# Five buffers in place of three for the raw halves of w_in's weights

## The chip, the core and the metric

The kernel runs on one core of a Trainium2 chip. The core has a matrix engine (PE, TensorE), a vector engine (DVE), a scalar engine (ACT), GpSimd (POOL) and a sync engine (SP), which here only issues transfers. Each takes its instructions in the order in which they stand in its own queue. A transfer is issued by SP's or ACT's queue and then carried out by 16 DMA engines that all queues share. The fast memory on the chip, SBUF, has 128 partitions; a buffer of it is given by its bytes per partition. The metric is the time of one execution in microseconds (us), as the median of several runs.

## The reference

One layer of a decoder for a prompt of 1024 rows and 64 sample rows (eight sequences of eight), with 1024 channels. It normalizes x and conditions it, projects it once, sends the parts of the projection through a pooling branch and a state-space (SSD) branch, and merges the two:

```python
shift, scale, gate = split(silu(c) @ w_ada + b_ada, 3)
h = rmsnorm(x, norm_g) * (1 + scale) + shift
u_pool, z_pool, z_ssm, xbc, dt_raw, g_raw = split(h @ w_in)     # one projection
p = (pool_mix(u_pool) * silu(z_pool)) @ w_pool_out
xs, B, C = split(silu(causal_conv(xbc)))
y = ssd(xs, softplus(dt_raw + dt_bias), -exp(a_log), B, C, state) + d_skip * xs
s = rmsnorm(y * silu(z_ssm), ssm_norm_g) @ w_ssm_out
m = sigmoid(g_pool) * p + sigmoid(g_ssm) * s
out = rmsnorm(x + gate * (m @ w_o), final_g)
```

All inputs and outputs are float32. The new states of pooling, convolution and SSD are outputs as well.

## The kernel before

**The projection.** h @ w_in is computed with h transposed: 1088 columns (1024 prompt rows and 64 sample rows), in halves of 544 and quarters of 272. The output channels of w_in go in pairs of 128 columns. Each pair is a two-by-two block product, carried out in the manner of Strassen with seven block products in place of eight (`strassen`). The blocks of the weight, b11, b12, b21 and b22, are the two halves of the 1024 input channels by the two column blocks of the pair.

**The loads in question.** For a pair, `pair_w` loads two raw tiles with the tag "rawA", one for each half of the input channels: 128 partitions by 4 KB. If the two column blocks are neighbours, a tile is one transfer of 512 KB (line 541); if not, two of 256 KB (line 544). They are issued by SP's queue. From the blocks, DVE and POOL make sums and differences (line 555; two more tiles with the tag "raw", called t3 and t2, and some in place in rawA). Each of the seven operands is then split into two parts of lower width that the matmul takes: ACT copies the high half (`whi`, line 166) and POOL, in the opening DVE, subtracts for the low half (`wlo`, line 169). `product` multiplies high by high, high by low and low by high, 128x272 each (lines 609 to 611), into PSUM, and DVE adds the results up (lines 620 and 625; tiles s1, u2, u3 and c2).

**Slots.** Tiles with one tag and in one pool take turns in a fixed number of buffers. The load of tile n waits until every reader of tile n-3 has finished; which is POOL's last wlo of it, as a rule. A load that waits on SP's queue holds up what stands behind it there: the stores of presplit weights (below), loads of convolution state (stc), of initial states, of the weights for the gate.

**The stages.** `first` makes the opening, up to about 107 us in the profile: x is loaded, its squares are summed (`x_square`, which uses a rawA tile as scratch), silu(c) @ w_ada gives the conditioning (`ada_out` uses a rawA tile too), h is made, and the first pair of the projection runs inside it. Its order is written out by hand. Then come the other pairs, to about 828 us, woven with their followers: convolution units (line 1057 on DVE), pooling units, outputs to DRAM through ACT (lines 721 and 723: activation and store). Beside them, a function `prep` splits the weights w_pool_out and w_ssm_out ahead of time: ACT's queue loads a block (pw, line 427, two buffers), ACT scales it (line 435) and makes the high half (ph, line 436), POOL the low half in place (line 438), and SP stores that (line 442, ws<-pw or wp<-pw). The last ten pairs run beside the SSD of the samples. The chunk stage, about 828 to 1178 us, works on the prompt's SSD in chunks of 128 rows. The tail applies w_o.

**What sets the order.** Outside the opening, a scheduler places each engine's instructions by priorities and by simulated times, in which the number of buffers counts. The order that results is fixed in the program.

**The pool.** rawA lies in the pool `pa`, with raw, s1, u2, u3, c2 and others, at the left end of SBUF; each tag follows the last one used before it. When the pairs are done, `pa` is closed and the pools of the chunk stage, `cl` and `ck`, are opened on the space. A tile of a new pool that lies on a tile of the old one waits for the last use of it: the framework adds the waits that are needed, one by one. In the chunk stage `ck` holds, among others, bt and btl (high and low half of B transposed, lines 1417 and 1444), xd and xw, xwl (x times dt; x times a decay in high and low half, lines 1426, 1429 and 1445), two of each.

Of the kernel before, what the change touches and what calls it, by code (L numbers as in the profile page):

```python
# [8 lines left out]
F32 = mybir.dt.float32  # L9
# [11 lines left out]
P = 128  # L21
D = 1024
# [24 lines left out]
def tile_pool_ssd_step(  # L47
# [9 lines left out]
    def nm(s):  # L57
        uid[0] += 1
        return f"{s}_{uid[0]}"
# [9 lines left out]
    def open_(name, bufs, side="left"):  # L69
        cm = tc.tile_pool(name=name, bufs=bufs, side=side, reuse_waits="tile")  # L70
        kept.append(cm)
        return cm.__enter__()
# [10 lines left out]
    pa = open_("pa", 1)  # L83
# [6 lines left out]
    def R(shape=(P, T), dt=F32):  # L90
        return hs.tile(list(shape), dt, tag="R", name=nm("R"), bufs=3)
# [71 lines left out]
    def split(raw, kept=None, ncols=P, eng=None):  # L163
        hi = wp.tile([P, 4, P], F32R, tag="whi", name=nm("whi"), bufs=4)
        lo = wp.tile([P, 4, P], F32R, tag="wlo", name=nm("wlo"), bufs=4)
        ins = act(hi[:, :, :ncols], raw[:, :, :ncols], AF.Copy)  # L166
        if kept is not None:
            kept.append(ins.ins)
        (eng or nc.gpsimd).tensor_tensor(lo[:, :, :ncols], raw[:, :, :ncols], hi[:, :, :ncols].bitcast(F32), ALU.subtract)  # L169
        return hi, lo  # L170

    def raw_(shape=(P, 4, P)):
        return pa.tile(list(shape), F32, tag="raw", name=nm("raw"), bufs=RAW)
# [28 lines left out]

    def x_square(i, eng):
        xt, n = xr[i]
        sqj = pa.tile([P, D], F32, tag="rawA", name=nm("sqj"), bufs=3)
        if eng is V:
            V.scalar_tensor_tensor(sqj[:n], xt[:n], 1.0, xt[:n], ALU.mult, ALU.mult, accum_out=ss[:n, i:i + 1])
        else:
            act(sqj[:n], xt[:n], AF.Square, accum_out=ss[:n, i:i + 1])
# [70 lines left out]
    def ada_out(part):  # L280
        a, b = PARTS[part]
        n = (b - a) * P // 2
        mr = pa.tile([P, 256], F32, tag="rawA", name=nm("mr"), bufs=3)
        act(mr[:, :n], pm[part][:, :n], AF.Copy)
        return mr

# [246 lines left out]
    def pair_w(c0, c1, pri, early):  # L533
        def run():
            with tc.high_priority(pri):
                raws = []
                for j in range(2):
                    r = pa.tile([P, 4, 2, P], F32, tag="rawA", name=nm("rawA"), bufs=3)
                    rows_ = w_in[0, j * 512:(j + 1) * 512]
                    if c1 == c0 + P:  # L540
                        load(r, rows_[:, c0:c0 + 2 * P].rearrange("(k p) (t c) -> p k t c", p=P, c=P))
                    else:
                        for t, c in enumerate((c0, c1)):
                            load(r[:, :, t], rows_[:, c:c + P].rearrange("(k p) c -> p k c", p=P))
                    raws.append(r)
            b11, b12, b21, b22 = raws[0][:, :, 0], raws[0][:, :, 1], raws[1][:, :, 0], raws[1][:, :, 1]
            w = []

            def add(x):
                with tc.high_priority(pri):  # L550
                    w.append(split(x, highs, eng=V if early else None))

            def diff(dst, x, y, op=ALU.subtract, eng=V):
                with tc.high_priority(pri):
                    eng.tensor_tensor(dst, x, y, op)  # L555

            def first_steps():
                t3, t2 = raw_(), raw_()
                diff(t3, b22, b12)
                diff(t2, t3, b11, ALU.add)  # L560
                yield
                add(b11)
                add(b21)
                diff(b21, t2, b21)
                yield
                add(b21)
                add(t2)
                yield
                add(t3)
                yield  # L570
                diff(b12, b12, b11)
                add(b12)
                yield
                add(b22)
                yield

            def steps():
                t3, t2 = raw_(), raw_()
                diff(t3, b22, b12)
                yield  # L580
                diff(t2, t3, b11, ALU.add)
                add(t2)
                add(t3)
                yield
                diff(b12, b12, b11)
                add(b12)
                add(b21)
                diff(t2, t2, b21, eng=nc.gpsimd)
                add(t2)
                add(b22)  # L590
                yield
            if early:
                return w, first_steps()
            add(b11)
            prep_q.append(steps())
            return w, prep_q[-1]
        return run
# [262 lines left out]
    def first():  # L860
# [51 lines left out]
        late = late_loads()  # L912

        x_square(0, V)
        x_square(1, V)
        c_turn()
        x_root(0, 2)
        x_unit(0, 2)
        x_square(2, None)
        x_square(3, V)  # L920
        x_turns(0, range(2))
# [21 lines left out]
        ada_mm(0, 6)  # L943
        ada_mm(0, 7)
        mr = ada_out(0)
        x_turns(2, range(5, 6))
        ada_end(0, mr)
# [15 lines left out]
        for k in range(4, 8):  # L963
            ada_load(2, k)
        next(late)
        mr = ada_out(1)
        products(2, range(1))
        ada_end(1, mr)
# [11 lines left out]
        for k in range(4, KT):  # L980
            ada_mm(2, k)
        mr = ada_out(2)
        products(2, range(3, 4))
        dtw = dt_w()
# [998 lines left out]
    for i in range(8):  # L1983
# [4 lines left out]
        r = R((P, D))  # L1988
# [65 lines left out]
```

## Time and profile before

| | |
|---|---|
| runs | 1292.78, 1290.96, 1286.81 us; median 1290.96 |
| profiled execution | 1292.2 us, its span 1290.4 us |
| mean granted clock of PE | 0.995 |
| 0 to 107 us (opening) | PE 95.26 of 107.00 us busy |
| 107 to 400 us (pairs) | PE 288.87 of 293.00 |
| 400 to 828 us (pairs, samples) | PE 420.67 of 428.00 |
| 828 to 1178 us (chunks) | PE 344.45 of 350.00 |
| 1178 to 1290 us (tail) | PE 105.83 of 112.00 |

The runs spread over 6 us. In the table the last five rows are from the windows of the trace. In rows of the timeline the columns are the start in us, the duration, the engine (with a q: its queue, for a transfer that it issues), the line, the operation, output<-inputs and, in square brackets, the idle time before it on its engine with what ended that. In rows of waits they are the waiting engine and line, what it waited for, and the total in us, the number of waits and the longest, or, for PE, the mean. A row of windows has the stretch, its length, busy us of PE, PE's weight loads, DVE, ACT and POOL with the number of instructions, the granted clock of PE, the share of the DMA engines and GB/s.

### The profile page before, as it was taken

How to read it: one execution, taken by the hardware profiler on the slowest of the kernel's cores; microseconds unless marked ns; L12 is line 12 of the kernel's file. 1: busy time of each engine (PE TensorE's matmuls, PEld its weight loads, DVE VectorE, ACT ScalarE, POOL GpSimd, SP SyncE). 2: the span in 40 equal slices, each digit the busy share in tenths (PEclk: the TensorE clock that was granted, in tenths of full speed). 3: DMA queues.
4: the chain of work that ended last, by engine and by line, in shares of the span. 5: the costliest groups of instructions: out<-in, count | busy, mean ns of one | idle time of the engine just before them, and what ended most of it. 6: DMA issues, size and time to landing. Idle time of an engine off the chain costs nothing. (4 is left out here: it accounts for less than half of the span.)

```text
span 1290.4 us, 26363 instructions
## 1 busy us (share of the span) xinstructions
PE 1255.1 (97%) x9771; PEld 1176.8 (91%) x9771; DVE 911.8 (71%) x1584; ACT 718.4 (56%) x1685; POOL 675.5 (52%) x555
## 2 busy tenths in 40 slices
PE   7999999999999999999999999999999999999997
PEld 6779999989999999999889999989999999989786
DVE  4686778865979588776667665488667879767533
ACT  4665356465556655554554564686887768522211
POOL 1007658678869777564344443446465656636000
PEclk9999999999999999999999999999999999999999
DMA  9736354465456453444546555889666666575431
GB/s 329 243 116 220 117 164 160 143 198 178 142 164 219 144 184 126 152 154 121 160 134 202 168 155 157 288 289 317 221 197 184 185 215 207 161 270 181 158 105 50
DMA packets 225730, 234.90 MB, mean 182 GB/s; under 512 B 30370, under 2 KB 177010, under 8 KB 225595
## 3 DMA queue, kind: packets, MB, share of 16 engines
q1 hardware_dynamic: 155808, 159.01, 39.6%
q10 hardware_dynamic: 69794, 74.22, 16.8%
q8 instruction: 77, 1.26, 0.4%
q14 instruction: 51, 0.41, 0.1%
HBM read 158.67 MB, written 74.62 MB: 181 GB/s over the span
## 5 line engine op out<-in xcount | busy, mean ns | idle before, releaser
L169 POOL TENSOR_TENSOR wlo<-rawA,whi 128x512 fp32r<-128x512 f32 x120 | 186.8, 1561 | 186.6 <-ACT whi L166 102.0
L169 POOL TENSOR_TENSOR wlo<-raw,whi 128x512 fp32r<-128x512 f32 x92 | 149.4, 1631 | 125.1 <-ACT whi L166 120.7
L360 PE MATMUL mm<-Y,whi 128*128 128x352 f32 (+1 forms) x480 | 160.0, 333 | 2.7 <-DVE G L1890 2.5
L361 PE MATMUL mm<-Y,whi 128*128 128x352 f32 (+1 forms) x480 | 157.8, 329 | 0.4 <-DVE Y L1516 0.4
L362 PE MATMUL mm<-Y,wlo 128*128 128x352 f32 (+1 forms) x480 | 157.3, 328 | 0.0
L611 PE MATMUL mm<-Y,wlo 128*128 128x272 f32 x496 | 143.7, 290 | 4.1 <-POOL wlo L169 3.6
L609 PE MATMUL mm<-Y,whi 128*128 128x272 f32 x496 | 146.4, 295 | 0.3 <-ACT whi L166 0.2
L609 PE MATMUL ps<-Y,whi 128*128 128x272 f32 x496 | 144.4, 291 | 2.2 <-ACT o L809 1.6
L610 PE MATMUL ps<-Y,whi 128*128 128x272 f32 x496 | 143.1, 289 | 0.0
L610 PE MATMUL mm<-Y,whi 128*128 128x272 f32 x496 | 142.8, 288 | 0.0
L611 PE MATMUL ps<-Y,wlo 128*128 128x272 f32 x496 | 142.6, 288 | 0.0
L166 ACT ACTIVATE whi<-rawA 128x512 fp32r<-128x512 f32 x125 | 78.0, 626 | 97.9 <-PE ps L610 43.2
L1057 DVE SCALAR_TENSOR_TENSOR GA<-GA,cvT,GA 128x1112 f32<-128x1112 f32 x72 | 126.4, 1758 | 0.3
L166 ACT ACTIVATE whi<-raw 128x512 fp32r<-128x512 f32 x96 | 58.8, 626 | 90.7 <-DVE raw L555 39.3
L611 PEld LDWEIGHTS mm<-Y,wlo 128*128 128x128 f32 x496 | 93.4, 188 | 6.0 <-POOL wlo L169 4.9
L609 PEld LDWEIGHTS ps<-Y,whi 128*128 128x128 f32 x496 | 93.3, 188 | 3.7 <-ACT o L809 1.8
L360 PEld LDWEIGHTS mm<-Y,whi 128*128 128x128 f32 x480 | 90.6, 189 | 5.5 <-DVE G L1890 3.5
L609 PEld LDWEIGHTS mm<-Y,whi 128*128 128x128 f32 x496 | 93.3, 188 | 2.4 <-ACT whi L166 0.9
L610 PEld LDWEIGHTS mm<-Y,whi 128*128 128x128 f32 x496 | 93.4, 188 | 0.7 <-issue 0.6
L610 PEld LDWEIGHTS ps<-Y,whi 128*128 128x128 f32 x496 | 93.3, 188 | 0.3 <-issue 0.2
L611 PEld LDWEIGHTS ps<-Y,wlo 128*128 128x128 f32 x496 | 93.5, 188 | 0.2 <-issue 0.2
L361 PEld LDWEIGHTS mm<-Y,whi 128*128 128x128 f32 x480 | 90.5, 189 | 2.6 <-DVE Y L1516 0.9
(459 smaller groups left out, 3842.8 us busy)
## 6 DMA issues: line engine op xcount, KB each, us to landing
rawA<-in_w_in SPq DMA_DIRECT2D x46, 512.0 KB
dec<-acs_d SPq DMA_DIRECT2D x32, 512.0 KB
xbc<-GA ACTq DMA_DIRECT2D x24, 512.0 KB
xb<-xbc SPq DMA_DIRECT2D x32, 384.0 KB
rawA<-in_w_in SPq DMA_DIRECT2D x32, 256.0 KB
pw<-in_w_ssm_out ACTq DMA_DIRECT2D x32, 256.0 KB
ws<-ph ACTq DMA_DIRECT2D x32, 256.0 KB
ws<-pw SPq DMA_DIRECT2D x32, 256.0 KB
```

The costliest lines, as they stand in the source:

```text
L166: ins = act(hi[:, :, :ncols], raw[:, :, :ncols], AF.Copy)
L169: (eng or nc.gpsimd).tensor_tensor(lo[:, :, :ncols], raw[:, :, :ncols], hi[:, :, :ncols].bitcast(F32), ALU.subtract)
L360: mm(ps[:, :n], a, rh[k][:, o:o + n], start=(k == 0), stop=False)
L361: mm(ps[:, :n], a, rl[k][:, o:o + n], start=False, stop=False)
L362: mm(ps[:, :n], b, rh[k][:, o:o + n], start=False, stop=(k == nk - 1))
L609: mm(p, hi, ah, start=(k == 0), stop=False)
L610: mm(p, hi, al, start=False, stop=False)
L611: mm(p, lo, ah, start=False, stop=(k == 3))
L1057: V.scalar_tensor_tensor(d[:, :n], rp[:, k:k + n], cvT[:, 24 * k + mc:24 * k + mc + 1], d[:, :n], ALU.mult, ALU.add)
```

## The change: five buffers for the tag rawA

The number of buffers of the tag "rawA" goes from 3 to 5, in the three places that name it. The same transfers, copies and products are made of the same sizes.

```diff
@@ x_square
-        sqj = pa.tile([P, D], F32, tag="rawA", name=nm("sqj"), bufs=3)
+        sqj = pa.tile([P, D], F32, tag="rawA", name=nm("sqj"), bufs=5)
@@ ada_out
-        mr = pa.tile([P, 256], F32, tag="rawA", name=nm("mr"), bufs=3)
+        mr = pa.tile([P, 256], F32, tag="rawA", name=nm("mr"), bufs=5)
@@ pair_w
-                    r = pa.tile([P, 4, 2, P], F32, tag="rawA", name=nm("rawA"), bufs=3)
+                    r = pa.tile([P, 4, 2, P], F32, tag="rawA", name=nm("rawA"), bufs=5)
```

Load n now waits for the readers of tile n-5. The pool `pa` grows by 8 KB per partition; the pools that are open beside it keep their places. What the scheduler makes of it is seen in the order of the queues. The number at a tile's name tells its instances apart.

On SP's queue, where the loads of the second and third pair stand in the opening (L839 are the gate's weights; rawA_1301 and rawA_1303 are the second pair's halves, rawA_1309 and rawA_1312 the third's):

```order
 L839 DMA gk_730<-in_w_ada 128x1024
 L541 DMA rawA_1301<-in_w_in 128x4x256
+L541 DMA rawA_1303<-in_w_in 128x4x256
+L544 DMA rawA_1309<-in_w_in 128x4x128 x2
 L839 DMA R_823<-in_w_ada 128x1024
 L839 DMA R_829<-in_w_ada 128x1024
```

Before, these two stood nine rows later, behind the gate's weights and other loads. Further on, too, each rawA load stands about two loads earlier; around 495 to 543 us of the profile, on SP's queue (ws<-pw are the stores of presplit weights):

```order
 L541 DMA rawA_6878<-in_w_in 128x4x256
 L442 DMA ws_213<-pw_6727 128x512
+L541 DMA rawA_7471<-in_w_in 128x4x256
 L442 DMA ws_214<-pw_6864 128x512
-L541 DMA rawA_7471<-in_w_in 128x4x256
+L541 DMA rawA_7473<-in_w_in 128x4x256
 L442 DMA ws_215<-pw_7039 128x512
+L541 DMA rawA_7479<-in_w_in 128x4x256
 L442 DMA ws_216<-pw_7176 128x512
-L541 DMA rawA_7473<-in_w_in 128x4x256
-L541 DMA rawA_7479<-in_w_in 128x4x256
```

The loads moved ahead of the stores ws_214, ws_215 and ws_216, by one store or two. On DVE, in the opening, the three differences of the second pair (raw_1323 is its t3, raw_1324 its t2) go to other places; one of them stands now between two steps of the first pair's operands:

```order
 L522 TENSOR_TENSOR tf_33_317<-tf_33_317,tf_24_290 128x544
+L555 TENSOR_TENSOR raw_173_1324<-raw_172_1323,rawA_162_1301 128x512
 L488 TENSOR_TENSOR R_142_1081<-tf_33_317,R_142_1081 128x544
 L625 TENSOR_TENSOR c2_134_1039<-s1_131_1036,mm_143_1084 128x272
```

It stood behind the results of the sixth and seventh product of the first pair. On POOL the steps of `prep` on pw (L438) move past low halves at six places; one of them:

```order
 L555 TENSOR_TENSOR raw_2995<-raw_2995,rawA_2836 128x512
+L438 TENSOR_TENSOR pw_3270<-pw_3270,ph_3396 128x512
 L169 TENSOR_TENSOR wlo_3068<-rawA_2834,whi_3067 128x512
 L169 TENSOR_TENSOR wlo_3072<-rawA_2836,whi_3071 128x512
 L169 TENSOR_TENSOR wlo_3077<-raw_2995,whi_3076 128x512
+L438 TENSOR_TENSOR pw_3404<-pw_3404,ph_3539 128x512
 L169 TENSOR_TENSOR wlo_3081<-rawA_2836,whi_3080 128x512
-L438 TENSOR_TENSOR pw_3270<-pw_3270,ph_3396 128x512
```

Each of the two stands three or four rows earlier. Last, ACT at the start of the chunk stage, printed with the waits of each instruction (DMAHW1 and DMAHW0 here are the stores of u2 and u3 of the last pair, the first being the L723 of the second row):

```order
 L721 ACTIVATE u_1850_10957<-u_1850_10957 128x272 [waits DVE_49] x2
 L723 DMA gs_148<-u_1850_10957 128x544 [waits DMAHW1_49,Activation_49]
-L1417 ACTIVATE bt_11239<-ps_11232 128x128 [waits DMAHW0_49,PE_49]
-L1429 ACTIVATE xw_11245<-ps_11231 128x512 [waits DVE_49]
+L1417 ACTIVATE bt_11239<-ps_11232 128x128 [waits PE_49]
+L1429 ACTIVATE xw_11245<-ps_11231 128x512 [waits DMAHW1_49,DMAHW0_49,DVE_49]
 L1402 ACT_TABLE_LOAD
 L1402 ACTIVATE cE_11248<-dec_11134 128x1024
```

No instruction moved; the tiles of `ck` lie 8 KB further along on what `pa` held. The wait for u3's store went from bt to xw, and a wait for u2's store was added to xw.

## The prediction, made before the changed kernel had run

> **What bounds the kernel now.** I began with the page's head, its busy shares and its list of DMA issues:
>
> ```profile
> span 1290.4 us, 26363 instructions
> PE 1255.1 (97%) x9771; PEld 1176.8 (91%) x9771; DVE 911.8 (71%) x1584; ACT 718.4 (56%) x1685; POOL 675.5 (52%) x555
> rawA<-in_w_in SPq DMA_DIRECT2D x46, 512.0 KB
> rawA<-in_w_in SPq DMA_DIRECT2D x32, 256.0 KB
> ```
>
> PE is busy for 97% of the span, so at most 1290.4 - 1255.1 = 35 us could ever come back, and only where PE waits for something that the weight loads set. The tag "rawA" is loaded by 46 whole and 32 half-sized transfers. Next I read the waits of SP's queue (sum, count, mean in us), since that is where a missing buffer shows:
>
> ```profile
> SPq L541 <- POOL wlo L169: 207.4, 37, 15.6
> SPq L544 <- POOL wlo L169: 58.8, 14, 9.4
> SPq L442 <- POOL pw L438: 98.6, 25, 11.3
> ```
>
> SP stands for 207.4 + 58.8 = 266 us in front of rawA loads whose buffer POOL has not yet released. That is large, but SP's waiting is no cost in itself; what counts is the same question asked of PE:
>
> ```profile
> PE mm L611 <- POOL wlo L169: 4.7, 8, 1.1
> ```
>
> Only 4.7 us in eight waits stand between POOL's low halves and PE, out of 266 us on the queue: nearly every late load is hidden. [...]
>
> The single waits, from PE's timeline (start, duration, instruction, idle time before it and its releaser):
>
> ```profile
> 107.03 0.40 PE L609 MATMUL mm<-Y,whi 128*128 128x272 f32 x1 [0.17 <-ACT whi L166]
> 108.72 0.39 PE L609 MATMUL mm<-R,whi 128*128 128x272 f32 x1 [0.41 <-ACT whi L166]
> 224.71 0.39 PE L611 MATMUL mm<-R,wlo 128*128 128x272 f32 x1 [0.90 <-POOL wlo L169]
> 526.38 0.40 PE L611 MATMUL mm<-Y,wlo 128*128 128x272 f32 x1 [0.46 <-POOL wlo L169]
> 530.40 0.39 PE L611 MATMUL mm<-Y,wlo 128*128 128x272 f32 x1 [0.71 <-POOL wlo L169]
> 543.21 0.36 PE L609 MATMUL mm<-G,whi 128*128 128x272 f32 x1 [0.67 <-DVE u L620]
> ```
>
> **Gains.** A load may now go out when the fifth-last buffer is free, not the third-last: about two loads earlier. I followed two of these waits back to a load (SP, DVE, ACT, POOL; then SP, DVE, DVE):
>
> ```profile
> 202.26 0.94 SPq L544 DMA_DIRECT2D rawA<-in_w_in  x2
> 208.45 1.74 DVE L555 TENSOR_TENSOR raw<-rawA,rawA 128x512 f32<-128x512 f32 x1 [2.25 <-POOL wlo L169]
> 212.89 1.15 ACT L166 ACTIVATE whi<-raw 128x512 fp32r<-128x512 f32 x2 [6.44 <-DMA xbc<-s]
> 222.31 4.69 POOL L169 TENSOR_TENSOR wlo<-rawA,whi 128x512 fp32r<-128x512 f32 x2
> ...
> 535.21 4.12 SPq L541 DMA_DIRECT2D rawA<-in_w_in  x2
> 539.19 0.69 DVE L555 TENSOR_TENSOR raw<-rawA,rawA 128x512 f32<-128x512 f32 x1 [6.74 <-DMA rawA<-in_w_in]
> 542.63 0.43 DVE L620 TENSOR_TENSOR u<-u,mm 128x272 f32<-128x272 f32 x1
> ```
>
> At 224.71 the load left at 202.26, DVE's difference came at 208.45 (its two inputs include that load; the releaser named had long been done), ACT's high halves 4.4 us later, and POOL fell behind. Two buffers more take this chain forward by far more than 0.90: gain **0.90**. At 543.21 PE waited for DVE's u, and DVE had stood 6.74 us for a rawA load: gain **0.67**. At 107.03 and 108.72 the halves of the second pair come late; the order has their loads ahead of the gate weights and two of ACT's copies ahead of the first pw load: gain 0.17 + 0.41 = **0.58**. At 526.38 and 530.40 POOL's step on pw stands ahead of the wlo that PE needs, because SP was held:
>
> ```profile
> 494.70 14.48 SPq L541 DMA_DIRECT2D rawA<-in_w_in  x2
> 509.23 1.06 SPq L442 DMA_DIRECT2D ws<-pw  x2
> 519.11 0.40 ACT L435 ACTIVATE pw<-pw,vT 128x128 f32<-128x128 f32 x1 [1.33 <-DMA pw<-in_w_ssm_out]
> ```
>
> SP stood 14.48 us at rawA loads, so the stores of pw left at 509.23, the buffers of pw came free late, and ACT waited for the next pw at 519.11. After the change the order has these stores behind fewer late loads. POOL keeps its work, so I take half of 0.46 + 0.71 = 1.17: **0.6**, bounds 0 and 1.17. Gains together 2.75; lower end 0, upper end 4.7 + 0.67 + 0.58 = 5.95, if every wait for POOL's wlo goes.
>
> **Losses.** First, DVE executes in order, and three L555 differences of the second pair move into the opening. One is now directly ahead of work that PE waits for:
>
> ```profile
> 88.57 0.72 DVE L522 TENSOR_TENSOR tf<-tf,tf 128x544 f32<-128x544 f32 x1
> 94.09 0.69 DVE L169 TENSOR_TENSOR wlo<-raw,whi 128x512 fp32r<-128x512 f32 x1
> 94.83 0.39 PE L611 MATMUL mm<-Y,wlo 128*128 128x272 f32 x1 [0.47 <-DVE wlo L169]
> ```
>
> The moved difference stands behind the row at 88.57, takes 0.69 (the row at 539.19), and the wlo at 94.09 already makes PE wait: cost **0.67**, bounds 0 (a gap of ACT's in between covers it) and 0.69. The two others, about 62 us, I cost at 0 because DVE idles for 3.40 - 1.33 = 2.07 and 3.50 - 2.55 = 0.95 us in the two windows ahead of them (quoted below); upper end 2 x 0.69 = 1.38, none below 0.
>
> Second, the pool that holds rawA grows by 2 x 4 KB per partition, and the chunk stage's pool is opened on the same space. xw (L1429) now lies on u2 and u3 of the last pair, whose stores (L723) are still under way; the order gives ACT's copy two DMA waits that it did not have. The end of the pairs (ACT, PE, DMA in 40 slices of 0.125 us from 833, DVE, PE; then another store of such a tile and the work behind it):
>
> ```profile
> 833.48 0.33 ACTq L723 DMA_DIRECT2D gs<-u  x1
> 834.08 0.59 ACT L1429 ACTIVATE xw<-ps 128x512 fp32r<-128x512 f32 x1
> 836.57 0.50 PE L1462 MATMUL ps<-xw,bt 128*128 128x512 f32 x1
> ...
> DMA  8899779958999999988821001000000000000006
> ...
> 843.54 0.28 DVE L1444 TENSOR_TENSOR btl<-ps,bt 128x128 fp32r<-128x128 f32 x1
> 843.97 0.25 PE L118 MATMUL ps<-identR,xb 128*128 128x128 f32 x1 [2.13 <-DVE btl L1444]
> ...
> 662.13 0.33 ACTq L723 DMA_DIRECT2D gp<-u  x1
> 667.07 0.44 DVE L620 TENSOR_TENSOR u<-s,mm 128x272 f32<-128x272 f32 x1 [6.15 <-DMA gp<-u]
> ```
>
> The store goes out at 833.48 and the DMA engines fall to nothing by slice 30, 833 + 30 x 0.125 = 836.8. So xw starts at 836.8 and not at 834.08: 2.7 later. Behind it in order ACT has a table load, cE, xD, the eight exponentials, bt and the copy into ps of the next chunk; DVE's mix and btl (843.54) wait for these, and PE for btl (843.97). I see nothing on ACT between that could absorb it, and PE is dense behind it (3.41 of 3.41 us in the window from 845.03, below): **2.7**. Bounds: 0, if the chain has slack that I miss, and 4.3, if the store takes as long as the 667.07 - 662.13 = 4.94 us of the other one (833.48 + 4.94 - 834.08).
>
> Third, PE's idle time at 843.97 grows from 2.13 to 4.8 us. The windows (busy PE, PEld, DVE, ACT, POOL, then the granted clock) around two such places:
>
> ```profile
> 53.10:56.50 3.40, 1.74 (x10) 1.20 (x10) 1.33 (x5) 1.76 (x4) 0.00 (x0) 1.00 0.44 130
> 56.50:60.00 3.50, 3.44 (x16) 3.14 (x16) 2.55 (x6) 3.43 (x7) 0.00 (x0) 0.51 0.26 93
> ...
> 841.60:845.03 3.43, 1.30 (x11) 1.18 (x11) 3.43 (x6) 3.41 (x11) 1.09 (x1) 1.00 0.95 261
> 845.03:848.44 3.41, 3.41 (x19) 3.03 (x20) 3.41 (x7) 2.90 (x10) 2.66 (x4) 0.50 1.08 356
> ```
>
> A window with 1.30 of 3.43, and one with 1.74 of 3.40, are followed by one at half clock. With PE idle until 846.7, the window 845.03 to 848.44 would have 848.44 - 846.7 = 1.7 busy, as little as these, so the next would run at half clock too: 3.41 x 0.5 = **1.7**; bounds 0 and 3.4 (two more). [...]
>
> Last, what moves on ACT, POOL and SP outside these places: ACT's early pw loads and scalings can block its copies, and the steps on pw stand ahead of a wlo on POOL in six places more; I take 0, since the DVE, ACT and POOL shares of 52 to 71% leave room, and price the other end below as a rival.
>
> **Sum**: 0.67 + 2.7 + 1.7 - 2.75 = +2.3 us. The profiled execution took 1292.2 (span 1290.4), which is 1.24 above the median 1290.96 of the runs: 1294.5 in its frame, **1293.3** as a median.
>
> **Rivals.**
> - Slower (chance 0.20). In six places POOL's step on pw (L438) now stands ahead of a wlo that stood ahead of it. The two waits at 526.38 and 530.40 are such a place: 1.17 us. Six of them cost 7.0, and with the sum above 1300.3. It decides (0.5%, 6.45 us, about what a measurement here can tell) from 4.15 / 1.17, four of the six. For it speaks that PE's waits for POOL are the largest of its waits for weights; against, that the steps come earlier because their pw came earlier, and that POOL is 48% idle.
> - All the gains and a covered transition (0.15): 5.95 less, 1285.0 to 1288 with the gains of 2.75. For it: ACT is 44% idle over the span. Against: the DMA activity up to 836.8 after a copy at 834.08.
> - Nothing reaches PE (0.10): the loads were hidden, the transition has slack: 1291, give or take 1. For it stands 4.7 against 266 us.
> - No second half-clock window (0.08). What decides then is that PE's idle time is split over two windows, each partly busy: sum +0.6, 1291.6. [...]
>
> **How the numbers follow.** The forecast holds 0.47. More than 0.5% slower come all of the first rival and a tail of the forecast of 0.03 (a longer store and two windows): 0.23. More than 0.5% faster needs all gains and something that I have not seen: 0.04, out of the second rival. Within 0.5%: 0.73. The range goes from 1285.5 to the first rival's 1300.5; the forecast's own is 1290 to 1297.
>
> **What the profile after would show.** Right: SP's waits at L541 and L544 for POOL well under 266 us; no waits at 224.71 and 543.21; xw (L1429) waiting some 2.7 us for the store of u; PE's wait for btl (L1444) near 4.8 us; two windows at half clock there. Wrong: xw starting right behind bt; PE's waits for wlo growing over 4.7 us, which would be the slower rival; or a half-clock window at a new place among the pairs.

## The result

The changed kernel takes 1286.53 us (median of 22 runs) against 1288.62 us of the kernel before (22 runs): a ratio of 0.9978, 95% interval 0.9971 to 0.9986. By the medians it is 2.1 us faster, by the ratio, which is an estimate of its own, 2.8 us (1.8 to 3.7), where the prediction said 2.3 us slower. Its profiled execution took 1286.55 us, at its median; the one shown of before, 1292.2 us, was 3.6 us above its own. The two traces differ by 5.6 us of span, more than the kernels do, and a second trace of before (first experiment) is used beside the first.

The head of the page after:

```profile
span 1284.8 us, 26355 instructions
PE 1254.1 (98%) x9771; PEld 1178.0 (92%) x9771; DVE 912.2 (71%) x1584; ACT 719.9 (56%) x1685; POOL 680.2 (53%) x555
```

The work is the same, 9771 matmuls; PE's share rose from 97 to 98%. To see where, I cut both executions at the same counts of PE's matmuls: the 871st, early in the second pair (which begins with the 848th), the 4371st, a matmul of line 1109 (the sixth of nine), the 6604th, the first of the sixteen ahead of the first product with xw (the 6620th), and the 6701st, in the chunk stage. Up to the 849th and behind the 957th PE's order in the trace is that of before; in the second pair the change puts 60 matmuls in other places, the 871st among them. The stretch from the 960th to the 4371st, where the order is the same, became 9.3 us shorter too (442.0 to 432.7). The windows between the first two cuts, for before and then for the changed kernel (length, busy us of PE, PE's weight loads, DVE, ACT, POOL with counts, clock, DMA share, GB/s):

```profile
110.69:563.84 453.15, 446.58 (x3503) 438.51 (x3501) 341.84 (x521) 248.77 (x593) 338.72 (x214) 1.00 0.51 165
```

```profile
111.24:555.11 443.87, 443.87 (x3502) 438.04 (x3501) 342.15 (x523) 250.39 (x595) 342.03 (x215) 1.00 0.53 169
```

453.15 us became 443.87, 9.3 less, and PE does not idle there at all any more. The changed kernel gave part of it back elsewhere. What SP's queue waits for (sum, count, longest; the third figure of every row of waits, PE's too, is the longest wait, and not the mean as the texts ahead of the result have it):

```profile
SPq L541 <- POOL wlo L169: 180.9, 36, 15.6
SPq L442 <- POOL pw L438: 122.9, 30, 13.0
SPq L544 <- POOL wlo L169: 52.2, 13, 10.1
```

SP still stands 233 us in front of rawA loads for POOL (before 266), and longer than before in front of the stores of pw (98.6 to 122.9): the queue got hardly freer. ACT got freer. Its waits for the presplit weights, before and then after:

```profile
ACT whi L166 <- DMA ws<-pw: 8.6, 2, 4.8
ACT pw L435 <- DMA pw<-in_w_ssm_out: 8.0, 7, 1.7
ACT ph L436 <- DMA pw<-in_w_pool_out: 3.9, 2, 2.8
```

```profile
ACT ph L436 <- DMA pw<-in_w_pool_out: 7.7, 3, 3.5
ACT pw L435 <- DMA pw<-in_w_ssm_out: 0.7, 2, 0.4
```

ACT no longer waits for the store of a pw that is to be overwritten (8.6 us in two waits), and hardly for the load of pw at line 435 (8.0 to 0.7); its waits for the blocks of w_pool_out, early in the pairs, grew (3.9 to 7.7) without a wait of PE. In the trace of before, the chain of the largest one reads as follows (SP's queue, ACT, PE):

```profile
243.72 0.39 SPq L541 DMA_DIRECT2D rawA<-in_w_in  x1
244.16 1.41 SPq L442 DMA_DIRECT2D ws<-pw  x2
...
249.44 0.95 ACTq L427 DMA_DIRECT2D pw<-in_w_ssm_out  x2
250.43 0.63 ACT L166 ACTIVATE whi<-rawA 128x512 fp32r<-128x512 f32 x1 [4.82 <-DMA ws<-pw]
...
262.89 0.39 PE L611 MATMUL mm<-Y,wlo 128*128 128x272 f32 x1 [0.69 <-POOL wlo L169]
267.50 0.39 PE L609 MATMUL ps<-Y,whi 128*128 128x272 f32 x1 [1.57 <-ACT o L809]
```

Two stores of pw leave only behind the held load of rawA. ACT's queue, which issues the next loads of pw, stands at them for 4.82 us, and with it everything that ACT should copy. 12 and 17 us later PE waits, once for a low half and once for an eviction (o) that ACT had not reached. In the changed kernel neither wait exists. That the one causes the other is so far read from the order; the experiments test it. The wait at 563 us has another such neighbour on SP's queue:

```profile
535.21 22.75 SPq L541 DMA_DIRECT2D rawA<-in_w_in  x3
558.06 0.45 SPq L1090 DMA_DIRECT2D s<-dts_d  x1
...
563.24 0.98 PE L1109 MATMUL ps<-ident,s 128*128 128x128 f32 x7 [0.72 <-DMA s<-dts_d]
```

Three rawA loads are held, the last until 557.96, and the load of s that PE's next stage starts with stands behind them; after the change they go out earlier.

What was lost lies at the start of the chunk stage (ACT, then PE, then the windows there):

```profile
828.72 0.60 ACT L1429 ACTIVATE xw<-ps 128x512 fp32r<-128x512 f32 x1 [3.71 <-DMA gs<-u]
...
829.38 0.50 PE L1462 MATMUL ps<-xw,bt 128*128 128x512 f32 x1 [1.90 <-ACT xw L1429]
838.61 0.25 PE L118 MATMUL ps<-identR,xb 128*128 128x128 f32 x1 [1.91 <-DVE btl L1444]
...
827.68:831.09 3.41, 1.72 (x6) 1.01 (x7) 1.74 (x4) 2.34 (x3) 0.00 (x0) 1.00 0.01 3
831.09:834.51 3.42, 3.42 (x13) 3.42 (x12) 1.48 (x3) 3.39 (x11) 1.09 (x1) 0.50 0.07 12
```

xw waits 3.71 us for the store of u, PE 1.90 us for xw, and the next window runs at half clock (0.50). One more was lost between the two stretches, at the one wait of PE for POOL's wlo that is left. It was 1.09 us long in before, where the clock stayed at 1.00; in the changed kernel (PE, then the windows):

```profile
605.69 0.51 PE L611 MATMUL mm<-Y,wlo 128*128 128x272 f32 x1 [1.88 <-POOL wlo L169]
...
602.39:605.81 3.42, 1.54 (x13) 1.32 (x12) 0.09 (x1) 1.37 (x6) 3.18 (x3) 1.00 0.60 165
605.81:609.23 3.42, 3.42 (x27) 3.05 (x27) 1.47 (x3) 3.34 (x8) 0.00 (x0) 0.50 0.52 153
```

In all, the trace of the changed kernel has four such windows, each 3.41 us at a clock of 0.50, ahead of its last work (56, 606, 831 and 1149 us), the first trace of before three (57, 668 and 845 us) and its second one (1151 us). An estimate from every run's span and granted clock (span times what the clock lacks to 1) says the same: 7.0 us of clock lost on the average of the changed kernel's 22 runs, 4.3 to 5.9 us in the four rounds of 68 runs of before that stand beside the experiments. So by this estimate some 1 to 3 us of the gain in the pairs went into such windows. In the opening the three moved differences are where the order put them (DVE), and PE waits more at the first pair (PE):

```profile
61.69 0.69 DVE L555 TENSOR_TENSOR raw<-rawA,rawA 128x512 f32<-128x512 f32 x1
63.28 0.69 DVE L555 TENSOR_TENSOR rawA<-rawA 128x512 f32<-128x512 f32 x1
90.28 0.68 DVE L555 TENSOR_TENSOR raw<-raw,rawA 128x512 f32<-128x512 f32 x1
...
81.92 0.39 PE L609 MATMUL mm<-Y,whi 128*128 128x272 f32 x1 [0.33 <-ACT whi L166]
82.77 0.40 PE L611 MATMUL mm<-Y,wlo 128*128 128x272 f32 x1 [0.32 <-DVE wlo L169]
95.52 0.40 PE L609 MATMUL mm<-Y,whi 128*128 128x272 f32 x1 [0.68 <-ACT whi L166]
96.51 0.39 PE L611 MATMUL mm<-Y,wlo 128*128 128x272 f32 x1 [0.48 <-DVE wlo L169]
```

The two waits at 107 and 108.7 us of before are gone.

### The profile page after: what moved, and what is told of

Same layout as the page of the kernel before. It is cut to its first block, busy times and chain, and to the rows that moved or that the text cites. A ratio compares the mean times of both kernels' runs of the same rounds, so it can differ in the third digit from the quotient of the medians.

```text
span 1284.8 us, 26355 instructions
## 1 busy us (share of the span) xinstructions
PE 1254.1 (98%) x9771; PEld 1178.0 (92%) x9771; DVE 912.2 (71%) x1584; ACT 719.9 (56%) x1685; POOL 680.2 (53%) x555
## 4 chain that ended last, share of the span: by engine, by line
PE 49%; DVE 1%; issue 1%; DMA 1%; ACT 0%; SPq 0%; POOL 0%; DVEq 0%; POOLq 0%; ACTq 0%
PE mm L360 6%; PE mm L361 6%; PE mm L362 6%; PE ps L1214 3%; PE ps L2000 2%; PE ps L2002 2%; PE ps L2001 2%; PE ps L609 2%; PE ps L611 2%; PE ps L610 2%; PE mm L611 2%; PE ps L1217 2%; PE mm L609 2%; PE mm L610 2%; PE ps L1295 1%
## 5 line engine op out<-in xcount | busy, mean ns | idle before, releaser
L169 POOL TENSOR_TENSOR wlo<-raw,whi 128x512 fp32r<-128x512 f32 x92 | 154.2, 1683 | 129.6 <-ACT whi L166 94.3
```

## Experiments

Two theories were set against each other for the gain. Theory P: a held load of rawA costs time by way of what stands behind it on SP's queue, above all the store of pw. Theory L, which is how the prediction read the waits at 224 and 543 us: the raw halves themselves come late. Theory A is the account of the two traces. For all kernels, the length of the stages that were cut as above, in us, one execution each:

| kernel | opening, first pair and start of the second, to the 871st matmul | pairs, 871st to 4371st | chunk start, 6604th to 6701st |
|---|---|---|---|
| before | 103.95 | 453.14 | 15.07 |
| before, second trace | 103.61 | 452.57 | 13.52 |
| changed | 104.65 | 443.87 | 17.34 |
| e_gap (before, 8 KB left empty) | 102.48 | 453.11 | 18.46 |
| e_places (five, chunk stage's places kept) | 102.48 | 444.25 | 13.52 |
| e_places_b (the same again) | 102.71 | 443.90 | 13.51 |
| e_places4 (four, places kept) | 101.81 | 446.80 | 13.51 |
| e_pw3 (three, three for pw) | 103.08 | 446.94 | 13.54 |
| e_free (three, stores of pw free) | 104.15 | 446.19 | 13.52 |
| e_places_pw3 | 104.05 | 444.09 | 13.51 |
| e_both | 104.12 | 444.02 | 15.09 |
| e_mid | 103.26 | 443.88 | 15.07 |
| e_hold | 103.98 | 443.88 | 16.87 |

The first column counts from the first matmul. A window at half clock (3.41 us at 0.50) adds 1.7 us where one falls, by the estimate 3.41 x 0.50: in the first column in before, changed, e_free, e_places_pw3 and e_both, in the last in before, e_both and e_mid, and in the three that wait for xw (two of them in e_gap).

**The kernel before, a second trace.** No edit.

> The kernel before, a second profile. Theory A (the waits follow from the order of the queues): PE waits again for whi, wlo, o or u near 224, 263, 267, 526, 530, 543 and 563 us, together about 6.5 us as in the first profile (0.90 + 0.69 + 1.57 + 0.46 + 0.71 + 0.67 + 0.72 = 5.7 of them at these seven places); the span is nearer to 1287 than to 1290, because the half-clock windows fall elsewhere. Rival B (they come and go with transfer times): fewer than four of the seven recur.

Its span is 1287.4 us. PE's waits in the stretch of the pairs:

```profile
PE mm L611 <- POOL wlo L169: 3.0, 5, 0.8
PE ps L609 <- ACT o L809: 1.5, 1, 1.5
PE ps L1109 <- DMA s<-dts_d: 1.1, 1, 1.1
PE mm L609 <- DVE u L620: 0.8, 1, 0.8
PE mm L609 <- ACT whi L166: 0.4, 1, 0.4
```

Six of the seven recur, within 1.7 us of their place; the one at 526 us does not, and two more of the first trace's ten do, at 291 and 555 us (6.3 us in all behind the 871st matmul, the wait for whi being ahead of it). So they follow from the queues' order. The 3.0 us by which this execution is shorter are about two half-clock windows, 1.7 us each by the estimate above: it has none of the three at 57, 668 and 845 us, and one at 1151 us.

**The chunk stage's places alone.** Three buffers and an empty gap:

```diff
-        sqj = pa.tile([P, D], F32, tag="rawA", name=nm("sqj"), bufs=3)
+        sqj = pa.tile([P, D], F32, tag="rawA", name=nm("sqj"), bufs=3); gap = i or pa.tile([P, 2 * D], F32, tag="gap", name="gap", bufs=1)
```

> Three buffers as before, and 8 KB left empty behind them, so that s1, u2, u3 and c2 and with them the chunk stage's tiles lie as in the changed kernel; the order of every queue is that of before. The trace of the changed kernel showed PE waiting 1.9 us for xw there: theory A expects +2 us (1.0015 of the time before), the prediction's own term +4.4 us (2.7 and a half-clock window, 1.0034), the rival that the chain has slack 0.

1293.73 us against 1289.17: 1.0030 (1.0019 to 1.0042), 2.4 to 5.4 us slower. The traces of this kernel and of before have the same order of PE, DVE, POOL and SP. The prediction's +4.4 lies inside, the +2 of theory A (the wait at PE alone) just outside. ACT, PE and three windows:

```profile
834.42 0.60 ACT L1429 ACTIVATE xw<-ps 128x512 fp32r<-128x512 f32 x1 [3.28 <-DMA gs<-u]
...
835.07 0.56 PE L1462 MATMUL ps<-xw,bt 128*128 128x512 f32 x1 [1.47 <-ACT xw L1429]
844.32 0.25 PE L118 MATMUL ps<-identR,xb 128*128 128x128 f32 x1 [2.34 <-DVE btl L1444]
...
832.00:835.44 3.44, 1.77 (x20) 1.17 (x19) 1.04 (x3) 1.00 (x2) 0.00 (x0) 0.99 0.17 62
835.44:838.85 3.41, 3.41 (x11) 2.88 (x10) 2.83 (x6) 3.37 (x7) 1.09 (x1) 0.51 0.02 5
845.68:849.09 3.41, 3.41 (x22) 3.02 (x23) 3.41 (x8) 2.90 (x9) 2.96 (x4) 0.51 1.08 348
```

The same wait for the store as in the changed kernel, with no other change, and two windows at half clock. So this cost is the tiles' new place, xw on u2 and u3. PE idles 1.47 + 2.34 = 3.8 us here where before has 2.13; the rest of the cost I put down to half clock, by the estimate of 1.7 us a window.

**Five buffers, the places kept.** The fourth and fifth buffer get a tag of their own that is first used behind c2, in the same turn of five; x_square and ada_out keep three:

```diff
+    highs, turn_w = [], [0]
+    half_tag, half_bufs = lambda: "rawB" if turn_w[0] % 5 > 2 else "rawA", lambda: (3, 3, 3, 2, 2)[turn_w.__setitem__(0, turn_w[0] + 1) or (turn_w[0] - 1) % 5]
...
-                    r = pa.tile([P, 4, 2, P], F32, tag="rawA", name=nm("rawA"), bufs=3)
+                    r = pa.tile([P, 4, 2, P], F32, tag=half_tag(), name=nm("rawA"), bufs=half_bufs())
```

> Five buffers in the same turn, but the fourth and fifth lie behind c2, so that the chunk stage's xw lies on them and not on u2 and u3. Theory A: no wait of xw for a store, 2 us faster than the changed kernel, 4 us faster than before (0.9968). Rival: the wait was covered, as fast as the changed kernel (0.9978).

1280.29 us against 1289.17: 0.9927 (0.9908 to 0.9946). Since that was more than the stages give, it was run once more:

> The kernel with the fourth and fifth buffer behind c2 once more, for its interval: 0.9927 (0.991 to 0.995) of the time before. If the first reading was lucky in its half-clock windows, 0.995, as with three buffers for pw.

1282.06 against 1288.60: 0.9957 (0.9940 to 0.9974), twelve runs. The points are 9.4 and 5.5 us, and the intervals barely meet; the expected 0.9968 lies in the second alone. The first reading was lucky in its half-clock windows: by the estimate from spans and granted clocks it lost 3.8 us to them where before lost 5.9, the second 5.5 where before lost 4.8. That is 2.8 us, as much as the two differ in the means of their runs (8.8 and 6.1 us faster); with the windows taken off both come to 6.8 us. Why this is less than the 9 us of the pairs was not found. The chunk stage starts in 13.5 us as in the undisturbed trace of before. This is the gain without the wait of xw. It is not the changed kernel in all else: in the opening three of its rawA loads leave 21 to 24 us earlier, and two differences of the second pair run 3 to 4 us earlier; with half-clock windows taken off, the two kernels differ there by 0.5 us or less (102.5 and 102.7 against 104.65 - 1.7).

**Three buffers for pw, three for rawA.**

```diff
-            raws[n] = gas[0].tile([P, 4, P], F32, tag="pw", name=nm("pw"), bufs=2)
+            raws[n] = gas[0].tile([P, 4, P], F32, tag="pw", name=nm("pw"), bufs=3)
```

> Three buffers for rawA as before, three in place of two for pw, so that ACT need not wait for the store of pw that stands behind a held load on SP. Theory P (a held rawA load cost time by way of the store of pw and ACT): the waits at 263, 267, 526 and 530 us go, 0.69 + 1.57 + 0.46 + 0.71 = 3.4 us less (0.9973), those at 224 and 543 stay. Theory L (the raw halves themselves came late): all stay, 0 (1.0000).

1283.63 against 1289.17: 0.9952 (0.9935 to 0.9968), more than the 0.9973 expected. Theory L falls for most of the time: with three buffers for the raw halves 5.6 to 6.2 us of the pairs' 8.7 to 9.3 are gone. Even the wait at 224 us, which theory P expected to stay, went; the wait for u near 543 stayed (0.9), and in place of the wait at 556 us there is one of 1.1 us for a wlo, 24 matmuls earlier. ACT still stands 7.1 us for loads and 4.9 us for stores of pw in this trace, so the sum of its waits is no price; what counts is when it reaches the copies that PE needs. Ahead of the two waits near 265 us, ACT's copies whi<-raw began at 260.81 us in before and begin at 254.41 here, of which 1.2 us are the opening's.

**The stores of pw freed.** One line of the source, with the buffers of before. It lets the scheduler place the store ahead of the last load that SP was given:

```diff
-            with behind(mybir.EngineType.SP):
+            with tc.high_priority(PRI):
                 load(jobs[n][2][:, 1], raws.pop(n))
```

> Three buffers for rawA, two for pw, as before; only the stores of pw (L442) no longer have to stand behind the last load that SP was given, so most of them stand one to three loads earlier on SP's queue. Theory P (the harm of a held load is the store behind it): the waits near 224, 262, 267, 291, 528 and 555 us go as with three buffers for pw, 0.995 of the time before; the wait for u near 543 stays. Theory L (the raw halves come late): nothing goes, 1.000.

1284.46 against 1288.60: 0.9969 (0.9953 to 0.9985); the expected 0.995 is just outside the interval, 1.000 clearly outside. In the order that the scheduler makes of it, some of POOL's steps on pw move ahead too, and 39 of PE's 9771 matmuls change places. PE's waits in the stretch of the pairs, and SP's queue at the place that the prediction followed from 202.26 to 224.71:

```profile
PE mm L611 <- POOL wlo L169: 1.1, 1, 1.1
PE ps L1109 <- DMA s<-dts_d: 0.6, 1, 0.6
...
197.17 0.36 SPq L442 DMA_DIRECT2D ws<-pw  x1
199.50 0.94 SPq L544 DMA_DIRECT2D rawA<-in_w_in  x2
```

In before, the store of pw left at 199.94 and the load 2.3 us behind it; here the store leaves at 197.17 and the load again 2.3 us behind it, with three buffers. So the two seem to hold each other: a held load delays a store, and by pw's buffers, ACT and POOL's step on pw the next load. The wait for u near 543 went too, against the expectation; in place of the one near 555 there is, as with three buffers for pw, one of 1.1 us.

How much earlier do the raw halves come? Counted by the matmul that PE is at when each of the 56 rawA transfers of the pairs leaves, the changed kernel is 103 to 234 matmuls ahead of before (median 177), this one between 7 behind and 28 ahead (median 3), and three buffers for pw about the same (median 1.5). In the 20 us ahead of the waits near 262 and 526 us they move by 9 matmuls at most, about 1.1 us. So at 262, 267, 526 and 530 us the store of pw and what follows from it is the cause, and hardly the late halves. Near 224 and 291 us the loads leave 2 to 3.5 us earlier as well, and there the two are not told apart. Behind the store, POOL's steps on pw and ACT's copies both come earlier (ACT's whi<-raw at 254.97 us in place of 260.81); no run parts these two.

**Four buffers.** As with five behind c2, with a turn of four (3 and 1).

> Four buffers in place of five, the fourth behind c2, so that the start of the chunk stage stays as before. Theory P (what costs is the store of pw that stands behind a held load): one buffer more is already enough to let most stores past, 0.994 to 0.996 of the time before. Theory L (the raw halves' own lateness): half of what five give, 0.9965.

1285.33 against 1288.96: 0.9967 (0.9955 to 0.9979). The time does not tell the theories apart; in the stage of the pairs it gives about what e_pw3 and e_free give (446.8 against 446.9 and 446.2), and the fifth buffer another 2.6 to 2.9 us.

**Five buffers and three for pw; five buffers and free stores.** Both edits are shown above.

> Five buffers behind c2 (as the kernel that leaves the chunk stage's places alone) and three for pw. Theory P: both take the same waits away, so nothing is added: 0.9927 of the time before, as with five buffers alone. Theory L (two separate gains): 0.9927 x 0.9952 = 0.988.

> Five buffers behind c2, and the stores of pw free of the last load as well. Theory P (the two act on the same queue and the same waits): the stretch of the pairs (from the start of the second pair to 563 us of before's profile) stays at the 444 us that five buffers give, 0.994 to 0.996 of the time before. Rival (the store's place and the load's lateness add up): 441 us there, 0.992.

1282.77 against 1288.96, 0.9952 (0.9938 to 0.9966), and 1280.63 against 1287.48, 0.9951 (0.9936 to 0.9965). Nothing is added: 444 us in the pairs, as with five buffers alone, where PE has no wait left that a second edit could take. The gains of the three edits are the same waits; more than that these two runs cannot tell.

**The differences held.** The second pair's three differences in the changed kernel may not go ahead of given instructions of DVE (the fifth and second last of the opening):

```diff
-                diff(t3, b22, b12)
+                diff(t3, b22, b12, at=x)
...
-                diff(t2, t3, b11, ALU.add)
+                diff(t2, t3, b11, ALU.add, at=y)
...
-                diff(b12, b12, b11)
+                diff(b12, b12, b11, at=y)
...
+    first(); dve = [i for i in nc.cur_bb.bb.instructions if i.engine == mybir.EngineType.DVE]; at_end.extend((dve[-2], dve[-5]))
```

> The changed kernel with the three differences of the second pair held on DVE to where they stood before (behind the results of the sixth product of the first pair). Theory A (the two differences near 62 us cost the opening, which the prediction put at 0): against the changed kernel the waits at 82 and 95 us shrink (0.33 + 0.32 + 0.68 + 0.48 there, 0.47 in all before), and the waits for whi at 107 to 109 come back (0.6): PE's first product of the second pair starts about 0.7 us earlier, its last one no earlier. Rival: the opening's shift is none of theirs, all four waits stay.

1288.93 us, a single execution. Three of PE's waits in its opening and first pair:

```profile
80.43 0.40 PE L611 MATMUL mm<-Y,wlo 128*128 128x272 f32 x1 [0.32 <-DVE wlo L169]
93.56 0.40 PE L611 MATMUL mm<-Y,wlo 128*128 128x272 f32 x1 [0.47 <-DVE wlo L169]
106.95 0.39 PE L609 MATMUL mm<-Y,whi 128*128 128x272 f32 x1 [1.37 <-ACT whi L166]
```

The wait for whi at 95 us is gone, as theory A had it, and the one at 107 us comes back with 1.37 in place of 0.6. Counted against the changed kernel from 59 us, where both have left the half-clock window that only one of them had, PE is 0.8 us ahead at the 752nd matmul and 1.2 us behind at the 860th. So in these two executions the early differences cost 0.8 us in the first pair and earn 2.0 at the second, and the expected "0.7 us earlier" of the second pair's first product was wrong: it is about 0.7 later. The size is not settled: from the 655th to the 847th matmul, other traces that hold the differences late and lack that window take 25.6, 26.2 and 26.3 us (e_gap, the second of before, e_pw3).

**The differences in between.** Five buffers behind c2, the three held to the 17th, ninth and second last of the opening.

> Five buffers behind c2, and the second pair's three differences held on DVE to places where DVE idled in the opening (0.70 us near 96) or at the end of the first pair. Theory A: the two at 62 us no longer push the opening, and the halves at 107 stay early: up to 1 us better than five buffers behind c2 alone, 0.992. Rival: no change that can be measured, 0.9927.

1282.56 against 1288.96, 0.9953 (0.9939 to 0.9966): no better than 0.9957 and 0.9927. The first pair is 0.9 us longer than in e_places (30.57 to 29.62 between the 655th and the 871st matmul).

## Why the prediction was wrong

- **What bounds the kernel.** PE is the bound, and SP's waiting is mostly hidden: that held, since 233 of 266 us of it are still there. Its reading of 4.7 us of waits for POOL's low halves as nearly all that reaches PE did not: the pairs became 9.3 us shorter in the trace (8.7 against the second trace of before).
- **Gains together 2.75, upper end 5.95.** This is the step that failed. All ten waits of PE in the pairs went, not three of them. Of the 9.28 us, 0.90 + 0.67 + 0.6 were foreseen in that stretch (the 0.58 at 107 us lies ahead of it and went as well). The missing part is: the other half of the 1.17 at 526 and 530 (0.6); 1.57 at 267.50, where PE waits for ACT's o, and 0.72 at 563.24, for the load of s, which I had not laid to rawA and which my upper end of "PE's waits for POOL's wlo" left out; four more waits for wlo, 1.56 in all, which I had in the upper end alone; and 2.7 us that are no idle time. The window of before has 6.57 us of idle PE in ten waits, but PE's busy time fell too, 446.58 to 443.87: some 0.27 us for each wait, besides what is shown in its brackets. In the five other traces with waits in this stretch it is 0.26 to 0.36 us.
- **"I take 0" for what moves on ACT, POOL and SP.** This was the term behind it. The early pw loads were taken as something that the change could only make worse. In fact the late stores and loads of pw were a cost of before, and e_free, which frees nothing but the stores of pw, has 6.4 to 7.0 us less in the pairs. The chain at 526 us in the prediction had this link (store behind load, pw late), and I halved it because POOL keeps its work.
- **The wait at 224.71.** It went as forecast, but the two buffers were not needed for it: the load stood behind a store of pw, and goes 2.8 us earlier when the stores are freed.
- **The DVE differences, 0.67 and 0.** In one execution the early ones cost about 0.8 and earn 2.0 at the second pair, against 0.67 and 0.58 in the sum. The opening as a whole came out near even, within what two executions differ by, and it decides nothing.
- **xw's wait, 2.7, and a second half-clock window, 1.7.** Right in place and about right in price: e_gap, which is this term alone, costs 3.9 us by its ratio (2.4 to 5.4) and 4.6 by the medians, against 4.4. The price is partly luck, since its parts were others. xw came late by 3.28 us of waiting, but PE's wait for btl did not grow from 2.13 to 4.8 us: in the changed kernel PE waits 1.90 for xw and 1.91 for btl, 1.7 more and not 2.7. The window stands behind the first of these (1.72 of 3.41 us busy, then 0.50); the changed kernel has one there and e_gap two, where before has one in its first trace and none in its second.
- **The rivals.** The slower one was wrong: PE's waits for POOL's wlo fell from 4.7 to 1.9 us. "All the gains and a covered transition" was nearest, with gains half as large again and a transition that is not covered. No run shows as a rule that idle time split over two partly busy windows spares the half clock, as the last rival has it; the changed kernel's wait for btl (2.19 and 2.72 us busy) and that of the second trace of before (2.33 and 2.38) are two cases, with the clock at 1.00 in the windows behind. The half-clock window at a new place among the pairs, which the prediction named as a sign of being wrong, came at 606 us.

## What to carry to other kernels

Most of what the held transfers cost here lay in what stood behind them in the queue: before more buffers are given to such a transfer, follow each transfer behind it to the engine that needs it, and try to let those pass first. Here one line that frees the order was worth more than two thirds of what 8 KB gave in the pairs (6.4 to 7.0 of 8.7 to 9.3 us). And the larger pool moved its other tiles, so that xw waited 3.71 us for a store: look at what the next stage lays on them, and put new buffers where their last use is early; with the added buffers behind the others, the kernel was faster than with them in front (0.9927 and 0.9957 of the time before, against 0.9978).

## What the runs showed of the hardware

PE's wait for btl was followed by a half-clock window in one trace of before and not in the other. In the first it lasts 2.13 us (the prediction shows that window, 1.30 of 3.43 us busy), and the next window runs at 0.50. The second trace:

```profile
841.48 0.26 PE L118 MATMUL ps<-identR,xb 128*128 128x128 f32 x1 [2.12 <-DVE btl L1444]
...
837.03:840.44 3.41, 2.33 (x17) 2.16 (x15) 1.66 (x2) 3.38 (x11) 0.24 (x1) 1.00 0.93 283
840.44:843.86 3.42, 2.38 (x15) 2.21 (x15) 3.42 (x7) 3.39 (x12) 1.50 (x2) 1.00 0.97 333
843.86:847.27 3.41, 3.41 (x40) 3.09 (x40) 3.41 (x6) 2.90 (x6) 3.17 (x4) 1.00 1.06 314
```

In the other two traces the half-clock windows are 3.41 us long and start whole steps of 3.413 us apart: 605.81 and 831.09 us in the changed kernel, 225.28 us or 66 steps, and 667.53 and 845.03 us in the first trace of before, 177.50 us or 52 steps. The windows above are laid back in such steps from the second trace's own one at 1151 us, so where they begin is an estimate. None of them is less than 2.33 us busy, since the wait, from 839.36 to 841.48 us, lies across an edge, and the clock stays at 1.00; that the edge is the reason was not shown. Windows in which PE was busy for half of the time were followed by half clock elsewhere: 1.77 busy of 3.44 us in e_gap, and 1.72 of 3.41 in the changed kernel. Nor does the busy share alone settle it. In the second trace of before, on the same grid:

```profile
662.95:666.36 3.41, 1.51 (x13) 1.29 (x11) 0.40 (x2) 0.28 (x1) 0.19 (x1) 1.00 0.59 211
666.36:669.78 3.42, 2.99 (x27) 2.64 (x28) 3.29 (x8) 1.63 (x3) 0.84 (x1) 1.00 0.01 2
```

PE was busy for less than in those two, and the clock stayed at 1.00; what else counts, these runs do not show. By the estimate of 1.7 us each, such windows, which come or not, make up some of the 5 to 11 us over which the runs of before spread in a round (granted clock 0.992 to 0.999); how much was not measured.
